# A 64-byte tile behind the attention, attention-projection weights 64 bytes above their operands, and a new lay-out of the recurrent stretch, in a hybrid decoder layer

## The chip, the cores and the metric

The kernel runs on one core of one Trainium2 chip. Its time is the device time of one execution in microseconds (us), taken as the median of several runs. A separate execution is recorded by the hardware profiler; its trace is what the views below are read from.

## What is computed

One decoder layer on x of 512 tokens by 1,024 channels, all float32, cut to what matters here:

```python
h = rmsnorm(x, norm_mix_g)
q, k, v, xr, gr, g_attn, g_rnn = split(h @ w_in)              # 7 x 1024 columns
A = diff_attention(q, k, v, ...)                              # 8 heads, two softmaxes each, causal
R = gelu(gr) * rg_lru(conv4(xr))                              # gated linear recurrence along the tokens
m = sigmoid(g_attn) * (A @ w_proj_attn) + sigmoid(g_rnn) * (R @ w_proj_rnn)
x = x + m @ w_out
x = x + square(relu(rmsnorm(x) @ w_up)) @ w_down              # 4096 wide
```

## The kernel before, in words

**Numbers.** Every float32 operand is kept as two float32r tiles, a high part (ScalarE rounds it: the names end in `hi`) and a low part (VectorE subtracts: `lo`). A product is three matmuls: high by high, high by low, low by high. Weights come in units of 4 x 128 rows by 256 columns (512 KB): SyncE's queue loads one into a raw tile, ScalarE casts it to `whi` (1,024 columns), VectorE makes `wlo`, and TensorE uses the pair. A matmul has a weight tile of 128 columns and a tile that moves past it, of 512 or of 256 columns (four bytes each).

**Stages on TensorE, in the order of the program.**

1. Norm and a first set of gates, then queries, keys and values with the attention of the 8 heads between them. In the projections of that stage the *weights* move (256 columns of `whi` and `wlo`), and the tokens `hT` are what is loaded.
2. The *recurrent stretch*, `recurrent` (L934): for the recurrence the products x and g (columns of `w_in`, moving tile `hT`, 512 columns), the gates (moving tiles `xh`, `xl`, weights `gw`), the attention's projection as seven Strassen products M1 to M7 for each of two halves (24 matmuls each with a moving tile of 256 columns: M1 to M4 read `aT`, M5 and M6 `af`, M7 `ag`), and the projection of the recurrence (moving tile `R`, 192 matmuls of 512 columns).
3. The output product with `w_out` (moving tile `mT`), then the MLP. The MLP's first product, `pl`, is plain: 96 matmuls with 512 moving columns of `h2` (L1894). After two matmuls with `s2`, for the norm, all the rest of the MLP is Strassen products of 24 matmuls with 256 moving columns (L1872): 1,176 that read `h2` (w_up) and 1,344 that read `us` (w_down). At seven of them, listed in `STEADY` (L1870), one more matmul of 384 columns goes ahead of the first. `pl` and the next seven products (`uq`, 1) and those of the first half of w_down (`dn`, (0, 0)), 336 matmuls of 256 columns in all, stand ahead of the first of these.

**What sets the order in the stretch.** TensorE's order in outline is written by hand (`seq`, L1412: x, g, y for the projection of the attention, t for gates, a, b, c for the projection of the recurrence, o for w_out). A planner, `Plan` (from L800 on), then lays out all tasks of TensorE, VectorE, ScalarE and SyncE's loads: each has a price, a latest time, and places that it takes (2 raw tiles, 4 units, 8 banks). It perturbs the ranks at random, keeps a lay-out that is not longer, and issues the tasks in the order of their start times. `MARGIN` (L930) is a spare time that it adds ahead of each TensorE task; a load is priced by its time to land (5.6 us for a unit at L952, L1085 and L1404; 2.5 us for the gates' weights at L1233). The MLP has a planner of its own that the change does not touch.

**Where tiles lie.** Tiles come from pools on a stack in each partition of SBUF. The pools `cp`, `wp` (units and raw tiles) and `hp` (`hT`, later `mT` and every second `us`) lie lowest; `sm` and the attention's `wk` come above them and are closed at L1438 and L1439; then `rp` (stretch) and later `fin` (`h2`, the other `us`, `x2`, two raw tiles, a fifth pair of weight tiles) start where `sm` started, at byte 85,568. A unit's tile is 64 floats longer than its data, and `weight_pair(shift)` (L75) sets the data `shift` bytes into it. Each block of 256 or 512 columns, and each weight tile of 128 columns, starts a multiple of 256 bytes from its neighbour, so one number per tile, the address modulo 256, holds for all of its matmuls.

Of the kernel before, what the change touches and what calls it, by code (L numbers as in the profile page):

```python
# [13 lines left out]
F32 = mybir.dt.float32  # L14
# [7 lines left out]
P = 128  # L22
# [17 lines left out]
def tile_block(ctx: ExitStack, tc: tile.TileContext, x, w_in, w_rga, w_rgx, w_pa, w_pr, w_o,  # L40
# [12 lines left out]
    def psum_pool(name):  # L53
        es_ps.close()
        return es_ps.enter_context(tc.tile_pool(name=name, bufs=1, space=bass.MemoryType.PSUM, reuse_waits="tile"))
# [226 lines left out]
    wb = Weights(1, 1)  # L282
# [644 lines left out]

    LANDS = {"PE": 0.17, "DVE": 0.09, "ACT": 0.09}
    HOPS = lambda x, t: 0.06 + (MARGIN if t.engine == "PE" else 0.0) if x.engine != t.engine else x.us - x.land + (0.116 if t.engine == "DVE" else 0.09)
    MARGIN = 0.5  # L930
    dve = lambda columns: 0.06 + 0.00106 * columns
    act = lambda columns: 0.09 + 0.00084 * columns

    def recurrent(rp):  # L934
        plan = Plan(raw=2, unit=4, bank=8)
        I = InOrder(nc.tensor)
        def pe(us, go, after, takes=()):
            t = plan.task("PE", us, go, after, takes=takes)
            return t
# [5 lines left out]
        class Unit:  # L945


            def __init__(self, src, shift, have=None, raw=None, of=None, after=()):
                self.raw, self.pair, self.of = raw, have, of
                self.held = plan.hold("raw"), plan.hold("unit")  # L950
                if of is None:
                    after = [plan.task("SP", 0.1, self.load, (), 5.6, takes=self.held[:1])]  # L952
                self.cast = plan.task("ACT", act(1024), self.high, after, takes=self.held[1:])
                self.low = plan.task("DVE", dve(1024), self.rest, (self.cast,))
                self.held[0].users += [self.cast, self.low]
                self.src, self.shift = src, shift
                if have or raw:
                    after[0].begun = -20.0
                if have:
                    self.cast.begun = self.low.begun = -20.0  # L960
# [119 lines left out]
        class Raw:  # L1080


            def __init__(self, src, into=None, after=()):
                self.t, self.src, self.held = into, src, plan.hold("raw")
                self.came = plan.task("SP", 0.1, self.load, after, 5.6, takes=() if into is not None else (self.held,))  # L1085

            def load(self):
                if self.t is None:
# [3 lines left out]
        def added(x, y, after):  # L1092

            t = plan.task("DVE", dve(1024), lambda: V.tensor_tensor(out=x.t, in0=x.t, in1=y.t, op=ALU.add), [y.came, x.came, *after])
            y.held.users.append(t)
            return t

        def projection_units(n):

            X = Raw(w_pa[n, 0], grown[n], ())  # L1100
            whole = lambda r, *after: Unit(None, 0, of=lambda: r.t, after=after)
            u = {"M1": whole(X, X.came)}
            yield "M1", u["M1"]
            yield "M2", Unit(w_pa[n, 2], 0)
            b1 = Raw(w_pa[n, 1])
            x = added(X, b1, [u["M1"].low, u["M1"].cast])
            u = whole(X, x)
            yield "M5", u
            b3 = Raw(w_pa[n, 3])
            y = added(X, b3, [u.low, u.cast])  # L1110
            m6 = whole(X, y)
            yield "M6", m6
            z = added(b1, b3, [x])
            u = whole(b1, z)
            b1.held.users += [u.cast, u.low]
            yield "M7", u
            u = whole(b3, b3.came)
            b3.held.users += [u.cast, u.low]
            yield "M3", u
            b2 = Raw(w_pa[n, 2])  # L1120
            y = added(X, b2, [m6.low, m6.cast])
            u = whole(X, y)
            sums_done.append(u)
            yield "M4", u
# [3 lines left out]
        def project(n):  # L1128
# [42 lines left out]
            for p, unit in projection_units(n):  # L1171
                fresh = p in ("M1", "M2", "M5")
                on = "Z" if p in ("M2", "M5", "M3") else "Y"
                if fresh:
                    held[on] = plan.hold("bank")
                need = {"M1": (), "M2": scaled[2:]}.get(p)
                if need is None:
                    need = [f[{"M5": 0, "M6": 0, "M7": 1, "M3": 2, "M4": 0}[p]] for f in formed] if p != "M4" else scaled[2:]
                t = pe(2.72, product(p, unit, fresh, on), [unit.low, prev[on], *need], [held[on]] if fresh else ())
                unit.used(t)  # L1180
                ys.append(t)
                if p in ("M1", "M5", "M6"):
                    i = {"M1": 1, "M5": 2, "M6": 3}[p]
                    live[i] = x = A_(copied(i, on), [t, qfree[qfree.n - 2] if qfree.n > 1 else None])
                    qfree.n += 1
                    posts = [x]
                elif p == "M4":
                    posts = [V_(gated(0, on), [t])]
                else:
                    i = {"M2": 1, "M7": 2, "M3": 3}[p]  # L1190
                    x = V_(merged(i, on), [t, live[i]])
                    qfree.append(V_(gated(i), [x]))
                    posts = [x]
                held[on].users += posts
                prev[on] = posts[-1]
        class Freed(list):
            n = 0
# [5 lines left out]
        gw, prior = {}, [dict() for _ in both]  # L1203
        OXs, OGs, gate_pes, Rs = [], [], [], []

        def chunk(j):
# [23 lines left out]
                V.tensor_tensor(out=gw[j][1], in0=gw["raw"], in1=gw[j][0].bitcast(F32), op=ALU.subtract)  # L1230

            graws = plan.hold("raw")
            load = plan.task("SP", 0.3, graw, [prior[0].get("glow")], 2.5, takes=[graws])  # L1233
            gh = A_(ghigh, [load, *prior[0].get("gates", ())])
            gl = V_(glow, [gh])
            graws.users += [gh, gl]
# [106 lines left out]
        for j in range(4):  # L1343
            chunk(j)
# [56 lines left out]
        w_o_first = []  # L1401
        for u in range(3):
            h = plan.hold("raw"), plan.hold("unit")
            load = plan.task("SP", 0.1, lambda: wb.fetch_one(), (), 5.6, takes=h[:1])  # L1404
            cast = plan.task("ACT", act(1024), lambda: wb.cast(lates), [load], takes=h[1:])
            low = plan.task("DVE", dve(1024), lambda: lates.pop(0)(), [cast])
            h[0].users += [cast, low]
            t = pe(5.44, lambda: None, [low, *w_o_first[-1:], *(m_done[4 * u:4 * u + 4] if u < 2 else ())])
            h[1].users.append(t)
            w_o_first.append(t)  # L1410
# [7 lines left out]
        assert not any(left.values()), {k: len(v) for k, v in left.items()}  # L1418
        wb.restart()
        slots[0] = 4  # L1420
        plan.run(dict(zip(("PE", "DVE", "ACT", "SP"), (*(0.0, 1.0, 1.0), 0.0))), 400)

    def gate(dst, js):
        for j in js:
# [12 lines left out]
    wb.pump()  # L1437
    es_at.close()  # L1438
    es_sm.close()  # L1439
    pp = psum_pool("ppb")  # L1440
    nb = {"acc": 8}
    with tc.tile_pool(name="rp", bufs=1, reuse_waits="tile") as rp:
        recurrent(rp)
# [85 lines left out]
    plan = []  # L1529
# [379 lines left out]
    for kind, a, p, pairs in steps:  # L1909
# [25 lines left out]
        after = [lows[o]]  # L1935
# [168 lines left out]
```

## Time and profile before

| What | Value |
|---|---|
| Median of 3 runs | 847.0 us (845.69 to 847.26) |
| Profiled execution, its own time | 845.23 us |
| Span of the trace, first to last instruction | 843.5 us |
| TensorE busy | 837.0 us, 99% of the span |
| VectorE, ScalarE, GpSimd busy | 685.8, 501.5, 99.3 us |
| Granted TensorE clock | 1.00 throughout |
| From the first product of the stretch to the end of w_out's loads (284 to 490 us) | 206.3 us |
| The MLP behind the norm's matmuls (542.20 to 839.63 us) | 297.43 us |

The busy time of TensorE is an upper reading: a row gives a matmul some 280 ns (256 columns) or 390 ns (512 columns) from its start until its results are out, while the next one starts after 113 to 120 ns or 227 to 236 ns. How fast TensorE goes is read from starts: a window that opens at one matmul's start and closes at another's, divided by the number of matmuls between them. I call that quotient the *pace*. The count that a window shows has one or two more, which began ahead of its left edge and are still under way.

### The profile page before, as it was taken

How to read it: one execution, taken by the hardware profiler on the slowest of the kernel's cores; microseconds unless marked ns; L12 is line 12 of the kernel's file. 1: busy time of each engine (PE TensorE's matmuls, PEld its weight loads, DVE VectorE, ACT ScalarE, POOL GpSimd, SP SyncE). 2: the span in 40 equal slices, each digit the busy share in tenths (PEclk: the TensorE clock that was granted, in tenths of full speed). 3: DMA queues.
4: the chain of work that ended last, by engine and by line, in shares of the span. 5: the costliest groups of instructions: out<-in, count | busy, mean ns of one | idle time of the engine just before them, and what ended most of it. 6: DMA issues, size and time to landing. Idle time of an engine off the chain costs nothing.

```text
span 843.5 us, 14702 instructions
## 1 busy us (share of the span) xinstructions
PE 837.0 (99%) x5788; PEld 774.2 (92%) x5788; DVE 685.8 (81%) x1100; ACT 501.5 (59%) x791; POOL 99.3 (12%) x126
## 2 busy tenths in 40 slices
PE   9999999999999999999999999999999999999998
PEld 7899999999888888988888887899999999999998
DVE  6766789988866398879897967999799769986996
ACT  7445477667665264767685446783587358545851
POOL 0041212323000100111110100000000001000000
PEclk9999999999999999999999999999999999999999
DMA  5346333433423432685867881545755655565563
GB/s 202 124 154 211 113 89 76 139 76 87 127 63 89 126 124 66 160 227 155 225 217 199 234 294 56 142 127 146 254 159 121 177 194 154 148 179 171 151 169 106
DMA packets 45620, 127.19 MB, mean 151 GB/s; under 512 B 8728, under 2 KB 13536, under 8 KB 45551
## 3 DMA queue, kind: packets, MB, share of 16 engines
q1 hardware_dynamic: 36144, 95.55, 35.4%
q0 software_dynamic: 9392, 30.69, 16.7%
q8 instruction: 45, 0.74, 0.3%
q14 instruction: 25, 0.20, 0.1%
q10 hardware_dynamic: 14, 0.01, 0.0%
HBM read 103.11 MB, written 11.06 MB: 135 GB/s over the span
## 4 chain that ended last, share of the span: by engine, by line
PE 86%; DVE 8%; ACT 3%; issue 2%; DMA 1%; SPq 0%; ACTq 0%; DVEq 0%
PE acc L70 58%; PE acc L152 6%; PE acc L153 6%; PE acc L154 6%; PE at L615 2%; DVE wlo L70 2%; PE at L152 1%; PE at L154 1%; PE at L153 1%; DMA wraw<-in_w_o_dram 1%; PE at L649 1%; DVE gate L70 1%; ACT whi L70 1%; PE at L546 1%; DVE pe L70 1%
## 5 line engine op out<-in xcount | busy, mean ns | idle before, releaser
L70 ACT CAST whi<-raw 128x1024 fp32r<-128x1024 f32 x109 | 112.1, 1048 | 99.4 <-DVE raw L70 41.8
L70 PE MATMUL acc<-h,whi 128*128 128x256 f32 (+1 forms) x851 | 159.6, 290 | 0.7 <-ACT h L70 0.5
L70 PE MATMUL acc<-us,whi 128*128 128x256 f32 x900 | 158.8, 280 | 0.0
L70 DVE TENSOR_TENSOR wlo<-raw,whi 128x1024 fp32r<-128x1024 f32 x109 | 131.0, 1219 | 20.1 <-ACT whi L70 20.1
L70 PEld LDWEIGHTS acc<-us,whi 128*128 128x128 f32 x900 | 137.9, 188 | 0.0
L70 PEld LDWEIGHTS acc<-h,whi 128*128 128x128 f32 x851 | 132.5, 188 | 4.3 <-ACT h L70 0.9
L70 PE MATMUL acc<-us,wlo 128*128 128x256 f32 x448 | 125.7, 280 | 0.0
L70 PE MATMUL acc<-h,wlo 128*128 128x256 f32 (+1 forms) x424 | 122.6, 289 | 0.0
L70 DVE TENSOR_TENSOR wlo<-wraw,whi 128x1024 fp32r<-128x1024 f32 (+2 forms) x84 | 95.2, 1145 | 27.8 <-ACT whi L70 27.3
L152 PE MATMUL acc<-whi,hT 128*128 128x256 f32 x384 | 109.3, 285 | 0.0
L153 PE MATMUL acc<-wlo,hT 128*128 128x256 f32 x384 | 107.5, 280 | 0.2 <-DVE wlo L70 0.2
L70 ACT CAST whi<-wraw 128x1024 fp32r<-128x1024 f32 (+2 forms) x84 | 81.7, 981 | 24.3 <-PE acc L70 11.9
L70 PEld LDWEIGHTS acc<-us,wlo 128*128 128x128 f32 x448 | 84.4, 188 | 0.0
L70 PEld LDWEIGHTS acc<-h,wlo 128*128 128x128 f32 x424 | 79.7, 188 | 1.6 <-DVE wlo L70 0.3
L154 PE MATMUL acc<-whi,hT 128*128 128x256 f32 x288 | 80.6, 280 | 0.0
L153 PEld LDWEIGHTS acc<-wlo,hT 128*128 128x128 f32 x384 | 72.6, 189 | 0.5 <-DVE wlo L70 0.4
L152 PEld LDWEIGHTS acc<-whi,hT 128*128 128x128 f32 x384 | 72.2, 188 | 0.5 <-issue 0.2
L70 PE MATMUL acc<-hT,whi 128*128 128x512 f32 x224 | 71.7, 390 | 0.0
L70 POOL TENSOR_TENSOR rs<-ms,mhalf 128x8 f32<-128x8 f32 (+1 forms) x25 | 39.1, 1564 | 201.2 <-DVE ms L70 200.9
L70 POOL DMA_DIRECT2D raw<-raw x24 | 20.7, 864 | 301.0 <-ACT q L70 115.5
L154 PEld LDWEIGHTS acc<-whi,hT 128*128 128x128 f32 x288 | 54.3, 188 | 0.0
L70 ACT ACTIVATE pe<-pe,nm 128x128 f32<-128x128 f32 (+3 forms) x64 | 35.6, 559 | 25.6 <-DVE nm L70 25.5
(241 smaller groups left out, 1830.1 us busy)
## 6 DMA issues: line engine op xcount, KB each, us to landing
wraw<-in_w_in_dram SPq DMA_DIRECT2D x54, 512.0 KB, 4.1
raw<-in_w_dn_dram SPq DMA_DIRECT2D x32, 512.0 KB, 4.1
raw<-in_w_up_dram SPq DMA_DIRECT2D x29, 512.0 KB, 4.3
raw<-raw POOLq DMA_DIRECT2D x24, 512.0 KB, 4.5
sum<-in_w_up_dram POOLq DMA_DIRECT2D x18, 512.0 KB, 5.5
wraw<-in_w_pa_dram SPq DMA_DIRECT2D x8, 512.0 KB, 3.7
wraw<-in_w_pr_dram SPq DMA_DIRECT2D x8, 512.0 KB, 5.5
wraw<-in_w_o_dram SPq DMA_DIRECT2D x8, 512.0 KB, 3.7
```

What stands on the lines that cost most here:

```text
L70: ins = f(*a, **k)
L152: T.matmul(o, l[0], r[0], start=first, stop=False)
L153: T.matmul(o, l[0], r[1], start=False, stop=False)
L154: T.matmul(o, l[1], r[0], start=False, stop=last)
L546: T.transpose(out=ps[:, t * P:(t + 1) * P], in_=qn[t // 2][:, c0:c0 + P], identity=ident)
L615: T.matmul(lg[c][:, :N], qT[:, c, i * P:(i + 1) * P], qk[h % 2, z][:, c, :N], start=z == 1, stop=z == 2)
L649: T.transpose(out=tp[:, b * P:(b + 1) * P], in_=st[s][:, b * P:(b + 1) * P], identity=ident)
```

## The change

**Addresses.** Behind the closing of `sm` and `wk` a pool with one tile of 16 floats (64 bytes) is opened and kept, so `rp` and `fin` start at byte 85,632 instead of 85,568. The units of the attention's projection get shift 128 instead of 0. The built programs have these addresses, modulo 256:

| Matmuls (count) | moving, before | weights, before | moving, after | weights, after |
|---|---|---|---|---|
| R, 512 columns (192) | 64 | 128 | 128 | 128 |
| gates `xh`, `xl`, 512 columns (48) | 64 | 64 | 128 | 128 |
| `aT`, 256 columns (192) | 128 | 64 | 128 | 192 |
| `af`, `ag`, 256 columns (144) | 64 | 64 | 128 | 192 |
| `pl`, `h2`, 512 columns (96) | 0 | 64 | 64 | 64 |
| MLP, `h2`, 256 columns (936 and 240) | 0 | 128 (936), 64 (240) | 64 | 128 |
| MLP, `us` in `fin`, 256 columns (540 and 132) | 0 | 128 (540), 64 (132) | 64 | 128 |
| MLP, `us` in `hp`, 256 columns (540 and 132) | 64 | 128 (540), 64 (132) | 64 | 128 |
| `hT`, `mT`, 512 columns | 128 | 128 | 128 | 128 |

In the MLP the counts of 240 and 132 are those whose unit lies in the fifth place, in `fin`; that place moves with the pool.

**Lay-out of the stretch.** `MARGIN` 0.5 becomes 0.8, a unit's load is priced 5.0 instead of 5.6, the gates' weights 5.4 instead of 2.5, and 1,200 perturbations are tried instead of 400. `seq` is the same.

```diff
-    MARGIN = 0.5
+    MARGIN = 0.8
...
-                    after = [plan.task("SP", 0.1, self.load, (), 5.6, takes=self.held[:1])]
+                    after = [plan.task("SP", 0.1, self.load, (), 5.0, takes=self.held[:1])]
...
-            whole = lambda r, *after: Unit(None, 0, of=lambda: r.t, after=after)
+            whole = lambda r, *after: Unit(None, 128, of=lambda: r.t, after=after)
...
-            yield "M2", Unit(w_pa[n, 2], 0)
+            yield "M2", Unit(w_pa[n, 2], 128)
...
-            load = plan.task("SP", 0.3, graw, [prior[0].get("glow")], 2.5, takes=[graws])
+            load = plan.task("SP", 0.3, graw, [prior[0].get("glow")], 5.4, takes=[graws])
...
-        plan.run(dict(zip(("PE", "DVE", "ACT", "SP"), (*(0.0, 1.0, 1.0), 0.0))), 400)
+        plan.run(dict(zip(("PE", "DVE", "ACT", "SP"), (*(0.0, 1.0, 1.0), 0.0))), 1200)
...
     es_sm.close()
+    ctx.enter_context(tc.tile_pool(name="apart3", bufs=1)).tile([P, 16], F32, name="apart3")
     pp = psum_pool("ppb")
```

The order changes in the stretch alone: the instructions are the same ones, and what stands before it and in the MLP keeps its order. On TensorE, at the last gates of the recurrence (`xh`, `xl` by `gw`) between the products of `R`, there stands before:

```order
L70 MATMUL acc_5054<-R_4901,wlo_4999 128x512
L70 MATMUL acc_5097<-xh_5044,gw0_5038 128x512
L70 MATMUL acc_5097<-xl_5045,gw0_5038 128x512
L70 MATMUL acc_5097<-xh_5044,gw1_5039 128x512
L70 MATMUL acc_5104<-xh_4965,gw0_5038 128x512
L70 MATMUL acc_5104<-xl_4966,gw0_5038 128x512
```

and now, where the first of the four gates comes:

```order
L70 MATMUL acc_5007<-R_4857,wlo_4960 128x512
L70 MATMUL acc_5056<-xh_5032,gw0_5041 128x512
L70 MATMUL acc_5056<-xl_5033,gw0_5041 128x512
L70 MATMUL acc_5056<-xh_5032,gw1_5042 128x512
L70 MATMUL acc_5062<-R_4478,whi_5036 128x512 x2
L70 MATMUL acc_5062<-R_4478,wlo_5037 128x512
```

Before, all four gates (12 matmuls) followed on each other; now one of them stands alone, with a product of `R` (24 matmuls) between it and the other three.

On SyncE's queue, at the start of the stretch (`in_w_in` for x and g, `in_w_pa` for the attention's projection, `in_w_rga` for the gates), there stands before:

```order
L964 DMA wraw_3787<-in_w_in_dram 128x1024
L964 DMA wraw_3834<-in_w_in_dram 128x1024
L964 DMA wraw_3879<-in_w_pa_dram 128x1024
L964 DMA wraw_3922<-in_w_in_dram 128x1024
L1090 DMA wraw_3967<-in_w_pa_dram 128x1024
```

and now:

```order
L964 DMA wraw_3792<-in_w_in_dram 128x1024
L964 DMA wraw_3836<-in_w_in_dram 128x1024
L964 DMA wraw_3880<-in_w_in_dram 128x1024
L964 DMA wraw_3917<-in_w_pa_dram 128x1024
L1090 DMA wraw_3966<-in_w_pa_dram 128x1024
```

The load for product M2 changed places with that of a unit of `w_in`, as the product itself moved behind 48 matmuls of `hT` on TensorE.

More of the change, by code (lines that the diff above doesn't have):

```diff
@@ L1084, in __init__ @@
                 self.t, self.src, self.held = into, src, plan.hold("raw")
-                self.came = plan.task("SP", 0.1, self.load, after, 5.6, takes=() if into is not None else (self.held,))
+                self.came = plan.task("SP", 0.1, self.load, after, 5.0, takes=() if into is not None else (self.held,))
             def load(self):
@@ L1403, in recurrent @@
             h = plan.hold("raw"), plan.hold("unit")
-            load = plan.task("SP", 0.1, lambda: wb.fetch_one(), (), 5.6, takes=h[:1])
+            load = plan.task("SP", 0.1, lambda: wb.fetch_one(), (), 5.0, takes=h[:1])
             cast = plan.task("ACT", act(1024), lambda: wb.cast(lates), [load], takes=h[1:])
```

## Prediction, made blind

> **What bounds the kernel now.** I read the page first, then windows by stage, then the waits of TensorE's weight loader. The page's busy times and granted clock:
>
> ```profile
> PE 837.0 (99%) x5788; PEld 774.2 (92%) x5788; DVE 685.8 (81%) x1100; ACT 501.5 (59%) x791; POOL 99.3 (12%) x126
> PEclk9999999999999999999999999999999999999999
> ```
>
> TensorE is busy throughout at the full clock. Three windows, with all engines for the first (us, busy time and count for PE, PEld, DVE, ACT, POOL, then clock, DMA share, GB/s) and TensorE alone for the other two:
>
> ```profile
> 542.20:839.63 297.43, 297.43 (x2528) 297.43 (x2526) 256.05 (x302) 175.25 (x225) 18.97 (x22) 1.00 0.57 162
> 518.00:542.20 24.20, 23.48 (x100) 1.00 0.33 92
> 284.00:490.30 206.30, 206.20 (x1062) 1.00 0.63 183
> ```
>
> In the MLP (first row) and in the stretch (third) TensorE has hardly an idle moment. Who held up its weight loads there, in the MLP and then in the stretch:
>
> ```profile
> PEld acc L70 <- DVE wlo L70: 0.3, 1, 0.3
> ...
> PEld acc L70 <- ACT tt L70: 0.7, 2, 0.5
> PEld acc L154 <- DVE wlo L70: 0.3, 1, 0.3
> ```
>
> So neither stage waits, and what can change the time is the pace at which matmuls start, and any new wait. The pace is not one number. Windows from start to start, TensorE alone, with my count of starts between their edges behind the fence:
>
> ```profile
> 44.03:52.51 8.48, 8.48 (x74) 1.00 0.43 142
> 66.76:73.56 6.80, 6.80 (x62) 1.00 0.79 246
> 232.79:234.21 1.41, 1.41 (x13) 1.00 0.02 1
> 90.86:93.35 2.50, 2.50 (x24) 1.00 0.00 0
> 310.26:321.15 10.89, 10.89 (x50) 1.00 0.47 144
> 360.01:365.66 5.65, 5.65 (x49) 1.00 0.70 176
> 336.24:339.11 2.87, 2.87 (x25) 1.00 0.52 184
> 441.05:469.05 28.00, 28.00 (x121) 1.00 0.72 198
> 544.93:556.31 11.39, 11.39 (x98) 1.00 0.56 186
> 684.57:686.61 2.04, 2.04 (x20) 1.00 0.96 277
> 612.96:615.32 2.36, 2.36 (x22) 1.00 0.13 50
> 587.31:597.87 10.56, 10.56 (x92) 1.00 0.79 231
> ```
>
> Take from each count the one or two that were already under way. In full-width matmuls (512 columns), `hT` at 128 over weights at 128 takes 10.89/48 = 227 ns (fifth row), and `R` at 64 over weights at 128 takes 28.00/120 = 233 ns (eighth). At 256 columns the offset of the weights from the moving tile, modulo 256, sorts them: 0 (`af`, seventh row) 2.87/24 = 119.6 ns; 128 (`h2`, ninth) 11.39/96 = 118.6; 192 (`aT`, sixth) 5.65/48 = 117.7. The offset 64 has two paces: weights of the query stage take 8.48/72 = 117.8 in the first row and 6.80/60 = 113.3 in the second, with the same addresses modulo 256 and the same lines of code; `h2` over the fifth unit takes 2.04/18 = 113.3 in the tenth and 2.36/20 = 117.8 in the eleventh. DMA traffic does not tell them apart: it is high in both rows of 113.3 that lie in projections, and nearly nil in the third and the fourth row, which differ all the same. I call them the fast and the slow pace. The last row alternates six matmuls at offset 64 with six at 128: 10.56/90 = 117.3, and each change costs the fast pace its start.
>
> What came ahead of a stretch at offset 64 decides which of the two it takes. The last matmul ahead of the third row and its first; then the last ahead of the fourth:
>
> ```profile
> 232.57 0.39 PE L154 MATMUL acc<-hT,wlo 128*128 128x512 f32 x1
> 232.79 0.28 PE L152 MATMUL at<-pt,v 128*128 128x256 f32 x1
> ...
> 90.32 0.34 PE L615 MATMUL at<-kl,qkT 128*128 128x384 f32 x1
> 90.50 0.28 PE L152 MATMUL acc<-whi,hT 128*128 128x256 f32 x1
> ```
>
> Behind full-width matmuls at 227 ns the third row is slow throughout, 1.41/12 = 117.8. Behind one of 384 columns the fourth is fast, 2.50/22 = 113.4, from three matmuls after it. Between a start and the next interruption neither pace turned into the other in the rows above.
>
> **The change, part by part.** The counts, as groups of instructions (busy time and the mean of one are their ends, not the pace):
>
> ```profile
> L70 PE MATMUL acc<-us,whi 128*128 128x256 f32 x896 | 158.3, 280 | 0.0
> L70 PE MATMUL acc<-us,wlo 128*128 128x256 f32 x448 | 125.7, 280 | 0.0
> L70 PE MATMUL acc<-h,whi 128*128 128x256 f32 x784 | 138.6, 280 | 0.0
> L70 PE MATMUL acc<-h,wlo 128*128 128x256 f32 x392 | 109.9, 280 | 0.0
> L70 PE MATMUL acc<-R,whi 128*128 128x512 f32 x128 | 40.3, 396 | 0.0
> L70 PE MATMUL acc<-R,wlo 128*128 128x512 f32 x64 | 25.3, 395 | 0.0
> ```
>
> *The MLP's 896 + 448 + 784 + 392 = 2,520 matmuls* all come to offset 64, moving at 64 over weights at 128, which is the query stage's pair of addresses. They and the seven of 384 columns take the 297.43 us of the window, 117.7 ns each. If all were fast: 2,520 x 113.3 = 285.5 and 7 x 0.17 = 1.2 (384/256 of a matmul), 286.7 us, a gain of 10.7. If all were slow: 296.9 + 1.2 = 298.1, a loss of 0.7. Which it is hangs on the entry. The first Strassen product follows full-width matmuls that will themselves sit at equal addresses, as ahead of the third row; I take it as slow, and its pace as held through 336 matmuls up to the first of the seven of 384 columns, which I take to do what the fourth row shows. The rest, 2,184, I take as fast, since the windows show no change of pace without an interruption and the MLP's waits are one of 0.3 us. Sum: 336 x 117.8 + 2,184 x 113.3 + 1.2 = 39.6 + 247.4 + 1.2 = 288.2, **a gain of 9.2** (bounds -0.7 and 10.7). What hides behind this is VectorE: 256.05 us of its work then stand in 288 instead of 297, 89% instead of 86%, and a unit's low part must be there every 24 x 113.3 = 2.72 us. If that cover fails, each wait costs itself and, at worst, the fast pace behind it: up to the next kick some 168 x 4.5 ns = 0.8 us.
>
> *R*, 128 + 64 matmuls, goes from 64 over 128 to 128 over 128, the fifth row's pair: 192 x (233.3 - 226.9) = **1.2**. *The plain product's 96* go from 0 over 64 to 64 over 64. The window of 518.00 to 542.20 is mixed with its entry, so I price them at R's old and new pace: 96 x 6.4 = **0.6**, between 0 and 0.6, since full width at 64 over 64 has only the 48 gates to show for it. *af and ag*, three of seven products, twice, 144 matmuls, come from 119.6 to offset 64 behind full-width gates or `hT`, so slow: 144 x 1.8 = **0.3** (0.9 if fast). *aT*, 192, from 117.7 to the slow 117.8: **0** (0.8 if fast). *The gates' 48* go from equal to equal addresses: 0, and I bound it by 48 x 6.4 ns = 0.3 either way.
>
> By the Trainium skill, "TensorE: Matmul & The Clock Gate" (Step-by-step: what each phase is for), weights and the moving tile come through two independent read ports of SBUF, and loading the next weights takes nothing from the running matmul. By it all these terms are nil; the trace does not agree, since 226.9 and 233.3 ns stand for the same shape at the same clock.
>
> *The lay-out* removes and adds no instruction. What it can win is the one place where TensorE stood, the gates that wait for ScalarE's `tt`, 0.7 us by the row above; there one gate now stands 24 matmuls ahead of the others, so I give its wait to the gain, but count as much for new ones: **0**. What it can lose is bounded by the loads, now priced at 5.0 to land. In the stretch (SyncE's issues, KB, median us to landing; the last row is min/median/max of all loads for the attention's projection):
>
> ```profile
> wraw<-in_w_in_dram SPq DMA_DIRECT2D x14, 512.0 KB, 4.7
> wraw<-in_w_pr_dram SPq DMA_DIRECT2D x8, 512.0 KB, 5.5
> wraw<-in_w_rgx_dram SPq DMA_DIRECT2D x4, 128.0 KB, 3.5
> ...
> DMA to landing us min/median/max: 3.4/4.4/8.6
> ```
>
> The `w_pr` loads land 0.5 us later than priced, and the spare of 0.8 ahead of each TensorE task covers that. A load at 8.6 would be 3.6 late, less 0.8: 2.8 us, bounds for the stretch -0.7 and some 3 us. The load moved behind one of `w_in` on SyncE's queue waits one issue more; the product that needs it moved too. On ScalarE, whose queue runs in order, every cast and `tanh` behind a late load waits with it, and TensorE's gates wait for these.
>
> Sum: 9.2 + 1.2 + 0.6 + 0.3 = 11.3, less 0.3 for what I cannot place: **11.0 us**. The profiled execution took 845.23 (span 843.5 and 1.7 around it), so 834.2 by its own time. It lies 1.8 under the median of the three runs; against that, 847.0 - 11.0 = **836.0**.
>
> **The rivals.**
>
> *The fast pace gets lost again and again.* Each wait, or the change from one product to the next, starts the choice anew, and half of the MLP is slow: 2,520 x 115.6 + 1.2 = 292.5, a gain of 4.9; with 2.1 from the rest 7.0, and **840.0**. For it: in the last of the windows the pace never settles, and a faster TensorE comes closer to VectorE. Against it: 60 and 72 matmuls on end held theirs across changes of unit.
>
> *The slow pace holds.* The entry is slow and 384 columns do not turn it: MLP +0.7, the rest -2.1, less 0.3 as above: **845.9**, within 0.2% (1.7 us), which is about what a measurement of this kernel can tell from no change. For it: the kicks have not been seen to act on a slow run in the MLP; where they stand before, the six matmuls behind them are at offset 64 for six only. Against it: the fourth row.
>
> *Addresses count for nothing*: the paces belong to the tiles and their stages, every term above is nil, and the time stays at **847.0**. (The rule of the two ports comes to the same.) Against it: the fifth unit's 113.3 and the other units' 118.6 are the same `h2` in the same stage.
>
> *Late loads stop the stretch*, the one that ends slower: the eight loads for the attention's projection, priced 0.6 lower than before, land at 8.6 and hold ScalarE's queue. At 2.8 us each 22.4, so 847.0 - 11.0 + 22.4 = **858.4**; it decides from the fifth of them on (14.0 against 11.0 + 1.7). Against it: their median is 4.4.
>
> **How the numbers follow.** The forecast 0.60, the lost pace 0.22, the slow pace 0.09, no effect 0.04, late loads 0.03; 0.02 for small waits of other kinds, which stay faster. Faster by over 0.2%: 0.60 + 0.22 + 0.02 + 0.01 of late loads too few to decide = 0.85. Within it: 0.09 + 0.04 = 0.13. Slower: 0.02. The range takes the forecast with all fast (1.5 for the first 336 and 0.8 + 0.6 for `aT`, `af`, `ag` at most: 833.1, which needs all of them; I set 833.5) and the lost pace with 2.5 us of waits (842.5): 0.82 of the chance.
>
> **What would show it.** In the changed profile the window of the MLP's 256-column matmuls should be 287 to 289 us with the first 336 at 117.8 ns and the rest at 113.3; `R` should start every 227 ns, `aT`, `af` and `ag` every 117.8. Each product alone tests its step. I am wrong if the MLP's pace stays over 116, if TensorE waits over 3 us in the stretch, or if a window at offset 64 changes pace in its midst without a wait.

## The result, and the profile after

The changed kernel takes 835.05 us (median of 4 runs, 834.05 to 836.0) against 846.35 for the kernel before (4 runs, 844.8 to 847.26). The ratio is 0.9868, 95% interval 0.9848 to 0.9888. The forecast was 836.0 within 833.5 to 842.5. The profiled execution took 834.05, with a span of 832.3: 11.2 less than the 843.5 of before. Two more profiled executions of the changed kernel are set beside these two below, since some of the differences are those of one execution.

The page's busy times and granted clock. TensorE is busy for 99% of the span, as before, and at the same clock, and VectorE's 684 us are the same work in a shorter span:

```profile
PE 824.7 (99%) x5788; PEld 762.8 (92%) x5788; DVE 683.8 (82%) x1100; ACT 500.5 (60%) x791; POOL 99.3 (12%) x126
PEclk9999999999999999999999999999999999999999
```

Windows by stage, with all engines (columns as in the prediction). The first is the MLP behind the norm's matmuls, the second the plain product `pl`:

```profile
541.11:828.46 287.35, 287.11 (x2528) 286.89 (x2526) 254.65 (x302) 174.74 (x225) 18.97 (x22) 1.00 0.60 167
516.82:541.11 24.29, 22.94 (x100) 18.24 (x99) 21.16 (x26) 17.40 (x31) 1.76 (x2) 1.00 0.33 94
```

The MLP went from 297.43 to 287.35 us: 10.1 of the 11.2. `pl` did not move (24.20 before). The stretch, from the first `aT` matmul to the first of `mT`, TensorE alone, first before and then after:

```profile
307.44:474.42 166.98, 166.88 (x890) 1.00 0.63 178
```

```profile
308.16:473.30 165.14, 164.84 (x889) 1.00 0.62 178
```

It gained 1.84. The rest is what lies outside these stages: the first `aT` comes 0.7 us later than before, and that arises in the first 11 us of the span, where the program was not changed; w_out's product is the same within 0.05.

Now the paces of the changed kernel (a pace is the time from one matmul's start to the next one's), in windows from one matmul's start to another's, TensorE alone. The starts between the edges are 336, 92, 92, 138, 284 and 336:

```profile
541.11:579.19 38.08, 38.08 (x338) 1.00 0.59 153
399.07:409.91 10.84, 10.84 (x94) 1.00 0.66 171
341.54:351.96 10.42, 10.42 (x95) 1.00 0.65 181
441.97:473.30 31.33, 31.33 (x139) 1.00 0.78 214
605.00:637.18 32.18, 32.18 (x286) 1.00 0.60 164
752.12:790.20 38.08, 38.08 (x338) 1.00 0.61 174
```

The first row is the MLP's first 336 Strassen matmuls: 38.08/336 = 113.3 ns, the fast pace from the start. The prediction had the slow one there. The second and third are `af`, `aT` and `ag`, all at offset 64: 10.84/92 = 117.8, slow as foreseen, and 10.42/92 = 113.3, fast. The fourth is `R`, 31.33/138 = 227.0. The last two, from further on in the MLP, are both 113.3.

Who held up TensorE's weight loads: first from `pl`'s first matmul to just behind the MLP's entry, then in the stretch, then in the rest of the MLP (us in total, times, longest):

```profile
PEld acc L70 <- ACT h L70: 1.5, 1, 1.5
PEld acc L70 <- DVE h L70: 0.5, 1, 0.5
...
PEld acc L70 <- ACT tt L70: 0.7, 1, 0.7
...
PEld acc L70 <- ACT q L70: 0.4, 1, 0.4
```

The first of them was shorter before:

```profile
PEld acc L70 <- ACT h L70: 0.9, 1, 0.9
```

So `pl` waits 0.6 longer for ScalarE's `h`. Its whole window is as long as before, so its 96 matmuls gained about as much. The gates still wait 0.7 for ScalarE's `tt`.

### The profile page after: what moved, and what is told of

The parts are those of the page before. It is cut to its first block, busy times and chain, and to the rows that moved or that the text cites. A ratio compares the mean times of both kernels' runs of the same rounds, so it can differ in the third digit from the quotient of the medians.

```text
span 832.3 us, 14697 instructions
## 1 busy us (share of the span) xinstructions
PE 824.7 (99%) x5788; PEld 762.8 (92%) x5788; DVE 683.8 (82%) x1100; ACT 500.5 (60%) x791; POOL 99.3 (12%) x126
## 4 chain that ended last, share of the span: by engine, by line
PE 76%; DVE 13%; ACT 5%; issue 3%; DMA 3%; SPq 0%; ACTq 0%; DVEq 0%
PE acc L70 48%; PE acc L152 6%; PE acc L153 6%; PE acc L154 6%; DVE wlo L70 4%; PE at L615 2%; DVE x L70 1%; ACT whi L70 1%; DMA wraw<-in_w_o_dram 1%; PE at L153 1%; PE at L154 1%; PE at L152 1%; DVE gate L70 1%; PE at L649 1%; DVE fs L70 1%
## 5 line engine op out<-in xcount | busy, mean ns | idle before, releaser
L70 PE MATMUL acc<-h,whi 128*128 128x256 f32 (+1 forms) x851 | 154.3, 285 | 1.6 <-ACT h L70 1.1
L70 PE MATMUL acc<-us,whi 128*128 128x256 f32 x900 | 153.3, 276 | 0.0
L70 PEld LDWEIGHTS acc<-us,whi 128*128 128x128 f32 x900 | 135.7, 188 | 0.0
L70 PEld LDWEIGHTS acc<-h,whi 128*128 128x128 f32 x851 | 130.6, 188 | 5.0 <-ACT h L70 1.5
L70 PE MATMUL acc<-us,wlo 128*128 128x256 f32 x448 | 123.7, 276 | 0.0
L70 PE MATMUL acc<-h,wlo 128*128 128x256 f32 (+1 forms) x424 | 120.8, 285 | 0.0
```

Source lines behind the costliest of these rows:

```text
L70: ins = f(*a, **k)
```

## The experiments

All times are medians, the ratio is to the kernel before in the same session. The stages of the traces (us; edges are matmul starts: first `aT`, first `mT`, first `h2`, first Strassen matmul of the MLP, last matmul) stand side by side. They are those of one profiled execution each, whose own time can lie off the median beside it: 834.05 for the changed kernel, 836.45 for its third time, 833.89 for the addresses alone, 849.05 at offset 128, 832.60 without the 384-column matmuls, 835.39 for four of 288 under the same plan. One of the seven added matmuls of 384 columns, or what stands in its place, is called a *kick*.

| Kernel | time | stretch | w_out | `pl` | MLP |
|---|---|---|---|---|---|
| before | 846.35 | 166.98 | 43.56 | 24.22 | 297.43 |
| after | 835.05 | 165.14 | 43.52 | 24.28 | 287.35 |
| after, second time | 835.51 | 165.59 | 43.64 | 24.88 | 288.86 |
| after, third time | 834.41 | 167.87 | 43.52 | 23.98 | 287.30 |
| addresses alone | 836.29 | 165.39 | 43.54 | 24.57 | 287.52 |
| lay-out alone | 845.68 | 167.44 | 43.56 | 24.18 | 297.43 |
| MLP at offset 128 | 846.74 | 167.59 | 43.52 | 23.85 | 300.16 |
| no 384-column matmuls | 838.59 | 166.53 | 43.52 | 23.06 | 286.50 |
| slow entry | 838.87 | 167.15 | 43.52 | 25.95 | 289.17 |
| slow entry, no 384s | 844.13 | 165.32 | 43.52 | 25.86 | 296.68 |
| four of 288, new plan | 836.09 | 166.39 | 43.52 | 24.28 | 289.40 |
| four of 288, same plan | 833.34 | 167.14 | 43.52 | 24.55 | 287.21 |

**Addresses alone and lay-out alone.** The first is the kernel before with these edits:

```diff
-            whole = lambda r, *after: Unit(None, 0, of=lambda: r.t, after=after)
+            whole = lambda r, *after: Unit(None, 128, of=lambda: r.t, after=after)
...
-            yield "M2", Unit(w_pa[n, 2], 0)
+            yield "M2", Unit(w_pa[n, 2], 128)
...
+    ctx.enter_context(tc.tile_pool(name="apart3", bufs=1)).tile([P, 16], F32, name="apart3")
```

The second is the changed kernel with the same three edits undone. Expected of the first:

> The 64-byte tile and the weights' shift of 128 are put into the kernel before; its lay-out of the stretch (0.5, 5.6, 2.5, 400) stays. Theory A, the addresses alone set the pace: the MLP's 256-column matmuls take 287.3 us as in the changed kernel, R starts every 227 ns, and the kernel is within 0.5 us of the changed one (835 us beside 846). Rival B, the new lay-out brings part of it: this kernel is 1 us or more slower than the changed one, and the difference lies in the stretch.

and of the second:

> The new lay-out of the stretch alone, with all tiles at the addresses of the kernel before. Theory A: no change, within 0.5 us of the kernel before (846 us), the MLP at 297.4 us. Rival B: 1 us or more faster than the kernel before, won in the stretch, which took 167.0 us from the first product of the attention's projection to the first matmul of the output product.

Measured: 836.29 us (833.89 to 837.68, ratio 0.9883, 0.9865 to 0.9902) and 845.68 (844.52 to 847.03, ratio 0.9988, 0.9976 to 1.0001). The stretch and the MLP of the addresses, then of the lay-out:

```profile
307.27:472.66 165.39, 165.29 (x890) 1.00 0.65 183
540.77:828.29 287.52, 286.99 (x2527) 1.00 0.59 167
```

```profile
307.53:474.98 167.45, 166.89 (x890) 1.00 0.62 176
542.72:840.15 297.43, 297.43 (x2528) 1.00 0.58 161
```

The addresses bring the MLP's 10 us by themselves, and 1.6 in the stretch of this trace. Their median lies 0.8 above that of the changed kernel in the same session (835.51, below), between the 0.5 and the 1 of the two theories, and the two ratios' intervals overlap. The lay-out brings nothing that can be told from no change, and its stretch is no shorter than before.

**The changed kernel again, twice.** Expected of the second and of the third time:

> The changed kernel once more, on the chip and beside the runs of the other three, so that differences of a microsecond among them can be read. All theories: 835 us, 0.987 of the kernel before.

> The changed kernel once more, beside the one with four added matmuls. Theory A: 835 us at the median, with runs from 832 to 837. Rival (its first median was luck): off by over 2 us.

Measured: 835.51 (832.15 to 836.83, ratio 0.9861, 0.9838 to 0.9884) and 834.41 (832.89 to 836.45, ratio 0.9861, 0.9844 to 0.9879). The second time's trace shows one cause of the spread. Windows of the MLP, TensorE alone, 331, 448 and 163 starts:

```profile
541.06:578.59 37.53, 37.53 (x333) 1.00 0.58 155
605.00:657.78 52.78, 52.78 (x450) 1.00 0.56 156
658.41:676.90 18.49, 18.49 (x165) 1.00 0.57 179
```

37.53/331 = 113.4, then 52.78/448 = 117.8, then 18.49/163 = 113.4. At 603.97 one matmul was followed by the next after 220 ns instead of 113 (the row below has two matmuls in one, and 0.50 less the 0.28 of one is the distance of their starts), and the pace behind it was the slow one, until the kick at 657.78.

```profile
603.97 0.50 PE L70 MATMUL acc<-h,whi 128*128 128x256 f32 x2
```

That is the rival of the lost pace, at work for 448 matmuls: 448 x 4.5 ns = 2.0 us. In the first trace a wait at the same place (514 and 223 ns at 603.90) left the pace fast.

**The MLP at offset 128.** The units' shift in the MLP is raised by 64 bytes:

```diff
-            units[o] = weight_pair((0 if own else 64) if o[0] != "pl" ...
+            units[o] = weight_pair((64 if own else 128) if o[0] != "pl" ...
```

> The changed kernel with the weights of the MLP's Strassen products 64 bytes further on, so 128 above what moves past them in place of 64; nothing else moves. Theory A, the offset sets the pace: 118.6 ns a matmul throughout, the MLP at 2,520 x 118.6 + 1.2 = 300.1 us, some 848 us in all. Rival D, the gain is due to where the moving tiles lie (all at 64 modulo 256): the MLP stays at 287 us.

Measured: 846.74 (844.84 to 849.05), ratio 1.0002, 0.9991 to 1.0013. The MLP:

```profile
543.28:843.44 300.16, 300.16 (x2528) 1.00 0.57 160
```

300.16 less 7 x 0.17 is 299.0/2,519 = 118.7 ns. One shift of 64 bytes, with the same tiles, stages and code, takes the whole gain away. So addresses count. That it is the difference that counts, and not the weights' own address, this run alone does not show, but other rows do: offset 128 takes 118.6 ns with the moving tile at 0 over weights at 128 (`h2` before) and 118.7 at 64 over 192 (here); offset 192 takes 117.7 at 128 over 64 (`aT` before) and 117.8 at 64 over 0 (fifteen offsets, below); and the paces 113.3 and 117.8 of offset 64 are found at 0 over 64, 64 over 128 and 128 over 192.

**Without the added matmuls of 384 columns.** The changed kernel with

```diff
-            if fresh and o in STEADY and u.start == 0:
+            if False and fresh and o in STEADY and u.start == 0:
```

> The changed kernel without the seven matmuls of 384 columns in the MLP; the order of all else stays. Theory A, the fast pace holds by itself as long as offset and stream stay as they are: 7 x 0.17 = 1.2 us less, the MLP at 286.2 us, 833.9 beside 835.1. Rival C, the seven restore a pace that is lost at each wait or change of operand: the stretches behind the two waits in the MLP, or behind the changes between h2 and us, fall to 117.8 ns; each 168 matmuls at that pace cost 0.75 us, and the kernel gets slower by 0 to 9 us.

Measured: 838.59, but from 832.6 to 843.77 in seven runs (832.6, 833.78, 836.33, 838.59, 842.13, 843.27, 843.77; ratio 0.991, 0.9873 to 0.9947). The profiled one is the 832.6, fast throughout, 286.5 us for the MLP.

```profile
540.51:827.02 286.51, 286.16 (x2521) 1.00 0.60 168
```

No trace shows one of 843; but 843.8 less 832.6 is 11.2, and some 2,180 to 2,520 matmuls at 4.5 ns more are 9.8 to 11.3, what a pace lost once early in the MLP and never found again would cost. The three runs over 842 had the full granted clock, so the clock does not explain them. So the seven don't pay where nothing goes wrong (MLP 0.85 shorter than in the changed kernel's first trace), and the time without them varied by 11 us; that a lost pace is the reason is argued and not shown, but the slow entry without the seven, below, shows that a slow pace does last.

**Slow entry, with and without them.** Six matmuls of 512 columns at equal addresses (128 over 128) ahead of the MLP's first Strassen product, their result overwritten:

```diff
             hi, lo = units[o]
+            if o == ("uq", 1, "M1"):
+                wide = h2.rearrange("p r i f s -> p (r i f s)")[:, 16:16 + 512]
+                for n in range(6):
+                    I.matmul(banks[b], hi[:, 0, :P], wide, start=True, stop=True)
```

> The changed kernel with six added matmuls of 512 columns at equal addresses (128 over 128) between the norm's matmuls and the first Strassen product; their result is overwritten. They add 6 x 0.227 = 1.4 us. Theory A, what stands ahead of a stretch at offset 64 chooses its pace: the first 336 matmuls are slow (117.8 ns, 1.5 us more), the first of the seven of 384 columns turns them fast, and the rest is at 113.3. Rival E, the pace behind the norm is fast whatever goes ahead (fast as in the changed kernel): 113.3 from the start.

And the same without the seven:

> The same six matmuls, and the seven of 384 columns left out. Theory A, a pace holds until something interrupts it: slow from the start, up to the first wait of TensorE in the MLP at least; if no wait comes, 2,520 x 117.8 = 296.9 us for the MLP. Rival E: 113.3 ns throughout, 285.6 us.

Measured, one run each: 838.87 and 844.13. With the seven (windows of 336 and 168 starts, up to the first added matmul and behind the third):

```profile
544.07:583.64 39.57, 39.57 (x338) 1.00 0.55 144
...
660.34:679.38 19.04, 19.04 (x169) 1.00 0.62 184
```

and without them, the whole MLP, 2,519 starts:

```profile
541.85:838.53 296.68, 296.68 (x2520) 1.00 0.58 161
```

39.57/336 = 117.8 up to the first 384 columns, then 113.3; and without them 296.68/2,519 = 117.8 to the very end. The kernel without the 384s takes 286.5 us for its 2,520 as it is, and 296.7 with six matmuls more ahead of them; and 10.2 is 11.2 (2,520 x 4.45 ns) less the 1.0 us of waits that only the first has. The first of the two is what the prediction had in mind for the changed kernel: 39.6 us up to the first added matmul. The second is its rival of the slow pace that holds (845.9), but for the kicks: where they are issued, they do turn it.

**Fifteen offsets.** Each of the MLP's 15 groups of seven products gets an offset of its own, with one added matmul of 384 columns ahead of each group; the units that `R` is multiplied by get others too:

```diff
-            units[o] = weight_pair((0 if own else 64) if o[0] != "pl" ...
+            at = OFFSETS[GROUPS.index(o[:2])] if o[0] != "pl" else 0
+            units[o] = weight_pair((at - 64) % 256 if own else at, fin if own else None)
...
+    OFFSETS = (64, 0, 16, 32, 48, 80, 96, 112, 128, 144, 160, 176, 192, 208, 224)
```

> The changed kernel with another offset of the weights in each of the 15 groups of seven products in the MLP (64, 0, 16, 32, 48, 80, 96, 112, 128, 144, 160, 176, 192, 208, 224 bytes above the moving tile, in the order of the program), one matmul of 384 columns ahead of each group, and eight offsets for the 24-matmul blocks of R (0, 32, 64, 128, then 224 and 160 by turns, 192, 96). Theory A: a smooth map with the fast pace of 113.3 ns around 64, between 117 and 120 at 0, 128 and 192, and 227 ns at 0 for the full-width R. Rival D, the paces belong to the tiles: no group differs from the others by its offset.

Measured: 847.54 (one run). Windows of 163 starts at offsets 64, 0, 16, 48, 112, 128, 192 and 208, in this order:

```profile
542.17:560.65 18.48, 18.48 (x166) 1.00 0.62 164
561.41:580.97 19.56, 19.56 (x166) 1.00 0.55 145
581.74:601.03 19.29, 19.29 (x166) 1.00 0.63 182
...
621.85:641.05 19.20, 19.20 (x166) 1.00 0.60 165
...
682.03:701.60 19.57, 19.57 (x166) 1.00 0.62 185
702.38:721.71 19.33, 19.33 (x165) 1.00 0.63 165
...
783.17:802.37 19.20, 19.20 (x166) 1.00 0.61 165
803.12:822.14 19.02, 19.02 (x165) 1.00 0.60 163
```

That is 113.4, 120.0, 118.3, 117.8, 120.1, 118.6, 117.8 and 116.7 ns a matmul; the ones left out lie between 116.6 and 120.0. Behind the same added matmul only offset 64 reaches 113.3, and its neighbours at 48 and 80 (117.8 and 118.7) do not, so it is not the smooth map that was expected. At full width it is the other way round: `R` in the same run, 24 matmuls at offset 192 and 24 at 96,

```profile
463.13:468.64 5.51, 5.51 (x25) 1.00 0.58 200
468.64:474.26 5.62, 5.62 (x25) 1.00 0.81 183
```

takes 229.6 and 234.2, and none of the seven other offsets tried beat the 227 of equal addresses.

**Which length sets the fast pace.** The seven are taken out. Ahead of each product that opens a bank stand six 512-column matmuls at equal addresses, which set the slow pace, and one of 0, 64, 96, ... 512 columns in turn:

```diff
-            if fresh and o in STEADY and u.start == 0:
+            if fresh and u.start == 0:
...
+                for n in range(6):
+                    I.matmul(first, hi[:, 0, :P], wide, start=True, stop=True)
+                cols = 32 * LENGTHS.pop(0)
+                LENGTHS.append(cols // 32)
+                if cols:
+                    I.matmul(first[:, :cols], hi[:, 0, :P], ..., start=True, stop=True)
```

> The changed kernel with its seven 384-column matmuls taken out; ahead of each Strassen product of the MLP that opens a bank stand instead six 512-column matmuls at equal addresses (they should make the pace slow, as six of them did at the MLP's entry) and behind them one matmul of 0, 64, 96, ... 480 or 512 columns in turn, at offset 64. Its results are overwritten. The time itself says nothing (the added matmuls cost some 1.5 us a product); read is the pace of the product behind each. Theory A (what decides between 113.3 and 117.8 ns is how the last matmuls ahead of a run stand in time, not a state that only a kick of 384 columns sets): 0 and 512 columns leave it slow at 117.8, 384 makes it fast at 113.3, and several other lengths do as well. Rival (an interruption of any kind makes the choice by chance): the same length is followed by both paces in different products.

Measured: 908.03, as the added work makes it. The windows behind 64, 128, 192, 256, 352 and 384 columns, with 126, 90, 127, 92, 91 and 91 starts:

```profile
672.29:686.58 14.29, 14.29 (x129) 1.00 0.44 138
820.15:830.75 10.60, 10.60 (x92) 1.00 0.37 92
577.03:591.43 14.40, 14.40 (x130) 1.00 0.43 128
724.07:734.91 10.84, 10.84 (x94) 1.00 0.35 87
748.27:758.99 10.72, 10.72 (x94) 1.00 0.43 101
628.88:639.20 10.32, 10.32 (x94) 1.00 0.33 77
```

113.4, 117.8, 113.4, 117.8, 117.8 and 113.4. Read behind all 45 of them: 0, 128, 160, 224, 256 and 352 columns leave it slow, 64, 96, 192, 288, 320, 384, 416, 448, 480 and 512 make it fast, each two or three times, with no exception. (For 512 columns the slow pace was expected.) The choice is not chance: behind a settled row of matmuls the length of the one between decides it. A longer one is not surer than a shorter (352 fails, 288 does it). And 512 columns make it fast when they are at offset 64, while six at equal addresses leave it slow, so full width as such is not what matters.

**Four added matmuls of 288 columns.** 288 columns take 0.13 us where 384 take 0.17, and one kick belongs behind the wait at 604:

```diff
-    STEADY = [("up", 2 * d, "M1") for d in range(1, 4)] + [("dn", (d, 1), "M1") for d in range(4)]
+    STEADY = [("up", 2, "M2")] + [("dn", (d, 1), "M1") for d in range(1, 4)]
```

> The changed kernel with four added matmuls of 288 columns in place of seven of 384: one behind the place at 604 us where the trace shows a wait (ahead of M2 of the third group of w_up's products), and one ahead of each of the last three second halves of w_down. Theory A (288 columns set the fast pace as 384 do; an added matmul costs 0.13 us instead of 0.17 to 0.18, and those that stand in runs already fast only cost): 0.7 us less where nothing loses the pace, and up to 2 us less where the wait at 604 us does, so between 832 and 835 us and a smaller spread. Rival (the seven are all needed): over 837.

Measured: 836.09 (835.35 to 837.63, ratio 0.9884, 0.9868 to 0.9900), not the 832 to 835 that my theory gave. The MLP's waits in it:

```profile
PEld acc L70 <- ACT whi L70: 1.5, 2, 1.2
PEld acc L70 <- DVE wlo L70: 1.0, 1, 1.0
```

The MLP's planner prices the added matmuls, and with others it laid VectorE's and ScalarE's work out anew. To test that, the same four were issued under the old plan (a list `KICKS` for what is issued, `STEADY` left for the prices), so that VectorE and ScalarE keep the changed kernel's order:

> The four added matmuls of 288 columns again, but the MLP's planner still priced for the seven of 384, so that VectorE and ScalarE keep the changed kernel's order word for word. Theory A (the kernel with four lost its 2 to 3 us to waits that the new plan of VectorE and ScalarE made, not to the four kicks): under 0.8 us of waits in the MLP, the fast pace nearly throughout, the MLP at 286.5 to 287.5 us, and a median of 833 to 835 us. Rival (TensorE, faster where kicks are missing, runs into VectorE whatever the order is): 2 to 3 us of waits again and 836 us or more.

Measured: 833.34 (832.42 to 840.46 in six runs, ratio 0.9862, 0.9832 to 0.9892). The loader's waits are gone but for one of 0.8 at 605 us, and that one lost the pace. Windows of 16 starts behind it, and of 258 behind the 288 columns at 608.96:

```profile
606.49:608.37 1.88, 1.88 (x18) 1.00 0.27 37
610.02:639.26 29.24, 29.24 (x260) 1.00 0.60 161
```

1.88/16 = 117.5 and 29.24/258 = 113.3. The kick behind the wait turned the pace back after some 25 matmuls, where the changed kernel, in its second trace, needed 448. The theory of the new plan holds, on one trace of each. The time cannot be told from the changed kernel's, though. One of the six runs took 840.46, and it has no trace; its granted clock was 0.996 where the others had 1.0 or 0.999, and 0.4% of 833 us is some 3 of its 7 us (an estimate), so the rest is open.

## Why the prediction was right, point by point

*What bounds it* held in the main: the pace of starts is nearly all of the time, and the waits of TensorE in the first trace are 0.6 us in the MLP and 0.6 in the stretch, read from the starts. Predicted gains against those of the two profiled executions, in us: MLP 9.2 and 10.08, stretch 1.5 (`R`, `af`, `ag`) and 1.84, `pl` 0.6 and -0.07, ahead of the stretch 0 and -0.7, w_out 0 and 0.04; sum 11.3 (11.0 with what I could not place) and 11.2. That the sum came out so close is luck: the MLP and the stretch gave 1.2 more than predicted, and `pl` and the first 11 us of the span 1.4 less. It is also one execution's: the MLP took 288.86 in the second trace and the stretch 167.87 in the third, 0.9 more than before.

*The MLP.* The step that failed is "the first Strassen product follows full-width matmuls that will themselves sit at equal addresses, as ahead of the third row; I take it as slow". It entered fast, 38.08 instead of 39.6 us, a gain of 1.5. What I left out of account is what stands between: the two matmuls with `s2`, which start 229 ns apart where `pl`'s start 226 to 227. I counted, in ten traces (all but those of the kernel before, the lay-out alone, the lengths and the same plan) and from the stretch on, the runs of 24 matmuls or more at offset 64. Behind 512-column matmuls that had settled at 225 to 227 ns in their last starts, 71 in 71 were slow; behind others, 11 were fast and 8 slow. So the entry was not of the kind that I took it for, but that the two `s2` matmuls made it fast is not shown: no run took them away. The MLP's own entry was fast in all seven traces that left it as it is. Against the 1.5 stand 0.6 us of waits at 603.90 and 797.11, which I had put at nothing. "I take as fast" for the rest held, since no pace was seen to change without an interruption; its fragility was real (the second time's trace), and the seven matmuls do what the fourth row had let me hope.

*R* was 227.0 instead of 233.3 ns, 1.2 us as summed. *af, ag, aT* were slow, but for the four products at 341 us (96 matmuls, 0.4 more), which stand behind three gates that had not settled. That place can go either way: in the eleven traces with the new order and the new addresses it was fast six times and slow five. *The plain product* gained its 0.6 in the starts of its matmuls and gave it back at its entry, where ScalarE's `h` was late: this is the one place where something else was late next, and I had named no cover for it. In the three traces where `R` runs at 232 to 233 ns (before, the lay-out alone, fifteen offsets) the first wait there, read from the starts (which give less than the loader's rows above: 0.65 for 0.9, 1.3 for 1.5), is 0.6 to 0.7 us; in the eleven where it runs at 227, ten have 0.8 to 2.1 and one none. That fits `R`'s earlier end leaving ScalarE and VectorE behind, but no run was made for it alone. *The gates' wait* for `tt` stayed at 0.7; setting one gate apart did not take it away.

*The lay-out* counted at nothing is confirmed at the median. Its traces show a weakness all the same: read from the starts, the two with the old order of the stretch wait 0.4 us there, the twelve with the new one 0.4 to 2.9, at gates that wait for VectorE's `q` and ScalarE's `tt` (2.0 and 1.2 in the loader's rows of the third time's trace below). Two traces of the old order are few, and the kernel with the old order and the new addresses is not faster. The eight late loads of the last rival did not come: 165.14 us for the stretch, and 167.87 in the longest of the changed kernel's three.

```profile
PEld acc L70 <- DVE q L70: 2.0, 1, 2.0
PEld acc L70 <- ACT tt L70: 1.2, 1, 1.2
```

*Addresses count for nothing* is refuted twice, by the two halves of the change and by offset 128. The rule of the Trainium skill that was weighed there ("TensorE: Matmul & The Clock Gate", Step-by-step: what each phase is for), that loading the next weights takes nothing from the running matmul, does not give the pace here: the same shape at the same clock took 113.4 to 120.1 ns by the offset of its weights alone. That the loading of weights is what slows the stream is not shown by that.

## What to carry to other kernels

When TensorE is busy all through at full clock, measure its time from start to start, group by the difference of the two SBUF addresses modulo 256, and shift one tile: here 64 bytes were worth 1.3% and cost nothing. A pace can have two values at the same addresses and keep the worse one for 300 us; look at what stands ahead of the run and behind each wait, and put a matmul there, of a length that has been seen to turn it. When an edit passes through a planner, keep the plan fixed in one experiment, or its reshuffling is taken for the edit's effect.

## What was not expected of the hardware

At 256 columns of float32r, offset 64 of the weights from the moving tile (modulo 256) alone has a pace of 113.3 ns; the fourteen others tried lie at 116.6 to 120.1. At 512 columns equal addresses are best of the eight offsets tried, 227 against 229 to 234. At offset 64 a second pace of 117.8 ns lasts as long as nothing interrupts it (2,519 matmuls, 297 us), and one matmul between sets which of the two follows, by its length: 64, 96, 192, 288, 320 and 384 to 512 columns give the fast one, none, 128, 160, 224, 256 and 352 the slow one. The shortest cost no less than a whole matmul of 256 columns: with 64, the next one started 31 ns later, but the one behind that only after 197. What in the chip makes these two steady states was not found, nor what decides behind a wait: waits of 0.1, 0.4 and 0.7 us kept the fast pace in some traces, and others of 0.1 and 0.8 lost it.
